# Three more feed-forward channels by seven half-products, in turns with their neighbours; thirteen low parts by adding transfers; the up pairs' weight sums on VectorE

## The chip, the cores and the metric

One core of one Trainium2 chip runs one layer of a hybrid decoder trunk (512 tokens, width 1024, fp32 in and out). The metric is device time of one execution in microseconds (us). A core has a matrix engine (TensorE, PE in the profile, whose weight loads are shown as PEld), a vector engine (VectorE, DVE), a scalar engine (ScalarE, ACT), a general engine (GpSimd, POOL), and SyncE (SP), which here only issues transfers. GpSimd issues transfers too (POOLq in the profile), the adding ones among them: such a transfer adds what it brings to what lies in the target.

## The reference, cut to what matters

```python
def reference(x, ...):
    u = rmsnorm(x, norm1_g)
    a_glu, q, k, v, r, g_low, gate_a, gate_b = split(u @ w_in)
    y_conv = ...          # gated unit, causal convolution of width 31, layer norm, swish, projection
    y_gla = ...           # gated linear attention in chunks of 64, projection
    h = x + (sigmoid(gate_a) * y_conv + sigmoid(gate_b) * y_gla) @ w_o
    u2 = rmsnorm(h, norm2_g)
    z = causal_conv3(u2 @ w_ffn_up) + b          # 2 x 2816 channels, width 3, each channel by itself
    h = h + (silu(z[:, :2816]) * z[:, 2816:]) @ w_ffn_down
    return rmsnorm(h, final_g)
```

The change lies nearly all in the feed-forward part: u2 @ w_ffn_up, the convolution of width 3, the gate, and the product with w_ffn_down.

## The kernel before, in words

**Products in three.** Every fp32 operand is split in a high part (rounded to the matrix engine's type) and a low part (the rest). One product of a 128-row block is three matmuls into the same bank (`mm3`, L448 to L450): activation-high by weight-low, low by high, high by high. A plain weight tile is 128 partitions by 1024 columns, eight blocks of 128, and serves one tile of 128 output channels for 512 tokens: 8 x 3 = 24 matmuls of 512 columns (`col_tile`). In `mm3`'s order the low part of the weight is needed from the first block on.

**How a weight gets ready.** `order` lists all weights in the order of use. SyncE loads each into one of four buffers (`raw_tile`). `weight()` hands over the next one and has the one two places further (`LOOK = 2`) made ready by `split_weight`: ScalarE writes the high part (`whi`, L355 for pairs, L385 for plain tiles), VectorE the low part (`wlo` = raw - high, L356 and L390). Some plain tiles outside the feed-forward part are in the set `ADDED`: for them ScalarE writes not only the high part but also minus the raw tile, rounded, as `wlo` (L387), and an adding transfer issued by GpSimd brings the weight once more onto it (L388), which leaves the low part.

**Seven for eight.** Two weight tiles p and q can be taken as a 2 x 2 matrix of half blocks and multiplied in seven half-size products instead of eight (`two_tiles`, with `step_of_two`): 7 x 4 blocks x 3 = 84 matmuls of 256 columns instead of 48 of 512. In the up stage the two tiles are a channel's value and gate tile (i, 22 + i), in the merge stage two channels of one gate. The operands are called x1 (1024 columns), x3 (1024), x2 (1024) and x4 (512): x1 serves `a11` and `a12`, x3 `n2` and `s1`, x2 `n3` and `s4`, x4 `a22`. Their sums of weights are four additions of 512 columns, made by GpSimd in `two_sums` (L327), three after x1's split and one after x3's, with a third raw buffer for the results. The partial results are copied by ScalarE (`put`, L1178) and combined by VectorE in two working tiles c1 and c2. The activations' side (`up_acts`, seven sums) is made once.

**The feed-forward stages.** 22 channels (tiles of 128) are taken in three groups, `GROUPS`, of four, three and four pairs. For each channel i there are two up tiles, i (value) and 22 + i (gate). Of each, `ffn_conv` makes the convolution of width 3: ScalarE the first tap with the bias (L1497), VectorE the other two (L1500). Then comes silu on ScalarE, and `gated` multiplies on VectorE. The first channel of a pair goes through `first_gated` and `first_of_pair`, the second through `second_of_pair` (VectorE sums L1541, L1542 and splits by `fsplit`, L1520). When a group's channels are there, `seven("w_down", ...)` multiplies them by the down matrix, by seven as well.

In every group, the second channels q of some pairs (6, 7; 10, 11, 21; 14, 15, 18) go by seven, and beside each the first channel f of a following pair (5, 8; 9, 20, 12; 13, 16, 17) by two plain tiles. `up_plan` writes out by hand the order of the two: in the middle of a group, f's two plain tiles a and b are cut in pieces and put between q's operands,

```python
seq = [x1, a1, x3, a2, x2, b1, x4, ("second", q), b2]   # then ("first", f)
```

so q's operands stand with wide products between them. The order of instructions on an engine otherwise follows from a scheduler, with some instructions tied by hand (`issue_after`, `keep_in_program_order`; `third_ahead` ties the making of the next x3 ahead of q's gate).

The merge stage earlier on (gates `w_gb` and `w_ga`, pairs (0, 1) to (6, 7)) uses the same `two_tiles` and `two_sums`.

Of the kernel before, what the change touches and what calls it, by code (L numbers as in the profile page):

```python
# [40 lines left out]
MERGE_REST = [("w_conv", m) for pair in O_PAIRS[2:] for m in pair]  # L41
LOOK = 2

ADDED = {("w_glu", 2 * k) for k in range(2, KT)} | {("w_r", m) for m in range(KT)}
ADDED |= {("w_v", KT // 2 + j) for j in (0, 1)}
RATE = 5.0
# [29 lines left out]
def trunk_layer(ctx: ExitStack, tc: tile.TileContext, a: dict, out: bass.AP):  # L76
# [60 lines left out]
    run64 = cp.tile([P, T], BF16, name="run64")  # L137
# [17 lines left out]

    def up_plan(gi):
# [8 lines left out]
        def unit(q, f, kind):  # L165

            a, b = f, FT + f
            x1, x3, x2, x4 = (("part", q, part) for part in ("x1", "x3", "x2", "x4"))
            a1, a2 = (("tile", a, ks) for ks in halves(4))
            if kind == "opens":  # L170
                b1, b2, b3 = (("tile", b, ks) for ks in halves(4, 6))
                seq = [a1, x1, a2, x3, b1, x2, b2, x4, ("second", q), b3]
            elif kind == "closes":
                a1, a2, a3 = (("tile", a, ks) for ks in halves(3, 6))
                seq = [x1, a1, x3, a2, x2, a3, x4, ("second", q), ("tile", b, whole)]
            else:
                a1, a2 = (("tile", a, ks) for ks in halves(5))
                b1, b2 = (("tile", b, ks) for ks in halves(4))
                seq = [x1, a1, x3, a2, x2, b1, x4, ("second", q), b2]
            return seq + [("first", f)]  # L180
# [143 lines left out]
    def two_sums(name, p, q, part):  # L324

        def add(out, x, y):
            work = nc.gpsimd.tensor_tensor(out, x, y, ALU.add)  # L327
            if name == "w_up":
                tc.keep_in_program_order(work)

        left, right = slice(0, T), slice(T, D)
        if part == "x1":
            one, two = pair_raws[name, p]
            three = raw_tile()
            pair_raws[name, p].append(three)
            add(three[:, left], one[:, left], two[:, left])
            add(three[:, right], three[:, left], two[:, right])
            add(two[:, left], two[:, left], two[:, right])
        if part == "x3":
            one, _, three = pair_raws[name, p]  # L340
            add(three[:, left], three[:, right], one[:, right])

    def split_weight(halves=False, between=None):

        if len(ready) < len(order):
# [4 lines left out]
            if name in SEVEN or name == "two":  # L350
                raw = operand(raw, *spec) if name in SEVEN else two_operand(*spec)
                n = raw.shape[-1]
                hi = wp.tile([P, D], F32R, tag="whi", name=nm("whi"), bufs=4)[:, :n]
                lo = wp.tile([P, D], F32R, tag="wlo", name=nm("wlo"), bufs=4)[:, :n]
                nc.scalar.copy(hi, raw)  # L355
# [18 lines left out]
            if halves:  # L374
# [9 lines left out]
                return [[lambda c=c, part=part: part(c) for c in cols] for part in (high, low)]  # L384
            nc.scalar.copy(hi, raw)  # L385
# [13 lines left out]
    def third_ahead():  # L399

        n = used[0] + LOOK
        if n == len(ready) < len(order) and order[n][0] == "two" and order[n][1][-1] == "x3":
            split_weight()
            return two_low[0]

# [46 lines left out]
    def col_tile(w, acts, acc=None, lo=0, hi=T, at={}, ks=range(KT)):  # L452
# [9 lines left out]
        return acc  # L462

# [707 lines left out]
    def two_tiles(name, p, q, acts7, side_bank, at_once=False):  # L1171

        x, y, z = mm_bank(), side_bank(), side_bank()
        c1, c2 = tmp(), tmp()
# [17 lines left out]
        w = weight("two", (name, p, q, "x3"))  # L1192
        step(x, "n2", w, 1, False)
# [299 lines left out]

    def ffn_conv(acc, m):
# [130 lines left out]
    for gi, pairs in enumerate(GROUPS):  # L1625
# [26 lines left out]
        for what, i, *rest in up_plan(gi):  # L1652
            if what == "tile":
# [3 lines left out]
                col_tile(wt, acts2, acc, ks=rest[0])  # L1657
                if KT - 1 in rest[0] and i < FT:
                    values[i] = value(i, acc)
            if what == "part":  # L1660
                if rest[0] == "x1":
                    units[i] = two_tiles("w_up", i, FT + i, lambda: up_acts, ax_bank)
                done = next(units[i])
                if done:
                    values[i] = value(i, done[0])
                    banks[FT + i] = (None, done[1])
                    third = [taps_at[0], third_ahead()]
# [108 lines left out]
```

## Time and profile before

| | |
|---|---|
| median of 3 runs | 825.51 us (824.53 to 825.88) |
| profiled execution | 826.27 us, of which its span is 824.5 us |
| mean granted TensorE clock | 0.999 |
| TensorE | busy 816.3 us, 99% of the span, 4323 matmuls |
| VectorE | busy 719.2 us, 87%, 1165 instructions |
| ScalarE | busy 449.8 us, 55%, 666 instructions |
| GpSimd | busy 148.9 us, 18%, 133 instructions |
| transfers | 106.27 MB, mean 129 GB/s |

The span is from the first to the last recorded instruction; the execution's own time is 1.8 us longer. A row of the trace gives the start (us), the duration (us), the engine, the line of the program, the operation, output <- inputs by the program's names, and the shapes. A row of a grouped view gives the same without the start, then xcount, the sum of busy time (us) and the mean of one (ns), then the engine's idle time ahead of them and what ended it. Durations of neighbours on one engine overlap a little, so the cost of one in a row is read from the starts.

### The profile page before, as it was taken

Reading aid. Unit: us, or ns where it says so; the run is one execution under the profiler, and the core shown is the slowest. Engines: PE = TensorE matmul, PEld = TensorE weight load, DVE = VectorE, ACT = ScalarE, POOL = GpSimd, SP = SyncE. Lnnn points to the kernel's source line nnn. Section 1 sums busy time; section 2 is a strip of 40 time slices with the busy share of each in tenths; the row PEclk is TensorE's granted clock in tenths of the full one; section 3 lists DMA queues with packets and bytes.
Section 4 is the critical chain, followed back from the end, with each engine's and each line's share of the span. In section 5 each row is a group of like instructions: output and inputs, shape, how many; then the busy total and the mean of one; then the engine's idle time right before and its main releaser. Section 6 shows DMA issues by size and latency. Waiting matters only on the chain.

```text
span 824.5 us, 11562 instructions
## 1 busy us (share of the span) xinstructions
PE 816.3 (99%) x4323; PEld 705.8 (86%) x4323; DVE 719.2 (87%) x1165; ACT 449.8 (55%) x666; POOL 148.9 (18%) x133
## 2 busy tenths in 40 slices
PE   9999999999999999999999999999999999999996
PEld 8888888888888889999988898898889988899885
DVE  5689999998989699886788889989975999789896
ACT  6744446655654456684454546556435663456654
POOL 2000010001010213443001100230123301622012
PEclk9999999999999999999999999999999999999999
DMA  8355673553443103323647633055642457334662
GB/s 317 94 118 150 153 184 103 128 153 103 89 116 103 51 27 114 116 78 106 211 112 215 177 101 103 27 167 160 143 132 89 140 142 164 105 103 148 184 128 103
DMA packets 30616, 106.27 MB, mean 129 GB/s; under 512 B 3464, under 2 KB 3600, under 8 KB 30560
## 3 DMA queue, kind: packets, MB, share of 16 engines
q1 hardware_dynamic: 24784, 85.34, 30.3%
q0 software_dynamic: 5760, 20.19, 14.4%
q8 instruction: 34, 0.56, 0.3%
q14 instruction: 22, 0.18, 0.1%
q10 hardware_dynamic: 16, 0.00, 0.0%
HBM read 103.42 MB, written 2.10 MB: 128 GB/s over the span
## 4 chain that ended last, share of the span: by engine, by line
PE 98%; DMA 0%; ACT 0%; DVE 0%; POOL 0%; POOLq 0%; issue 0%; ACTq 0%
PE mm L448 28%; PE mm L449 28%; PE mm L450 28%; PE mm L662 3%; PE ax L450 2%; PE ax L449 2%; PE ax L448 2%; PE ax L1067 1%; PE ax L576 1%; PE ax L1048 1%; PE ax L1069 1%; PE ax L1035 1%; DMA x<-in_x_dram 0%; PE ax L529 0%; PE ax L1033 0%; PE ax L1082 0%
## 5 line engine op out<-in xcount | busy, mean ns | idle before, releaser
L448 PE MATMUL mm<-uh,wlo 128*128 128x512 f32 (+1 forms) x672 | 244.8, 364 | 0.0
L449 PE MATMUL mm<-ul,whi 128*128 128x512 f32 (+1 forms) x672 | 242.6, 361 | 0.0
L450 PE MATMUL mm<-uh,whi 128*128 128x512 f32 (+1 forms) x672 | 242.3, 361 | 0.0
L450 PEld LDWEIGHTS mm<-uh,whi 128*128 128x128 f32 x672 | 126.9, 189 | 19.4
L448 PEld LDWEIGHTS mm<-uh,wlo 128*128 128x128 f32 x672 | 127.0, 189 | 18.8
L449 PEld LDWEIGHTS mm<-ul,whi 128*128 128x128 f32 x672 | 127.1, 189 | 18.6
L385 ACT CAST whi<-raw 128x1024 fp32r<-128x1024 f32 x86 | 89.7, 1046 | 57.6 <-PE mm L450 29.7
L356 DVE TENSOR_TENSOR wlo<-raw,whi 128x1024 fp32r<-128x1024 f32 x80 | 95.0, 1195 | 24.4 <-ACT whi L355 20.5
L327 POOL TENSOR_TENSOR raw<-raw,raw 128x512 f32<-128x512 f32 x42 | 67.7, 1613 | 211.8 <-DVE wlo L356 116.4
L390 DVE TENSOR_TENSOR wlo<-raw,whi 128x1024 fp32r<-128x1024 f32 x70 | 91.7, 1313 | 14.6 <-ACT whi L385 14.6
L355 ACT CAST whi<-raw 128x1024 fp32r<-128x1024 f32 x80 | 76.3, 957 | 36.2 <-PE mm L450 27.3
L786 DVE SCALAR_TENSOR_TENSOR c<-h,pp,c 128x255 f32<-128x255 f32 (+14 forms) x120 | 57.1, 476 | 3.2 <-ACT c L782 3.0
L786 DVE SCALAR_TENSOR_TENSOR c<-aside,btmp,c 128x255 f32<-128x255 f32 (+14 forms) x120 | 57.1, 476 | 0.0
L786 DVE SCALAR_TENSOR_TENSOR aside<-h,pp,aside 128x255 f32<-128x255 f32 (+6 forms) x112 | 53.3, 476 | 0.0
L355 ACT CAST whi<-kept 128x1024 fp32r<-128x1024 f32 (+1 forms) x32 | 31.8, 996 | 33.6 <-DVE kept L310 16.8
L1500 DVE SCALAR_TENSOR_TENSOR tmp<-mm,pp,tmp 128x511 f32<-128x511 f32 (+1 forms) x56 | 41.4, 743 | 4.0 <-ACT tmp L1497 3.9
L356 DVE TENSOR_TENSOR wlo<-kept,whi 128x1024 fp32r<-128x1024 f32 (+1 forms) x32 | 37.0, 1155 | 5.2 <-ACT whi L355 5.0
L1178 ACT COPY tmp<-mm 128x256 f32<-128x256 f32 x48 | 17.6, 367 | 34.2 <-PE mm L450 33.6
L1416 DVE TENSOR_TENSOR hres<-hres,mm 128x512 f32<-128x512 f32 (+1 forms) x49 | 32.3, 672 | 4.0 <-PE mm L450 2.6
L1497 ACT ACTIVATE tmp<-mm,pp 128x512 f32<-128x512 f32 x28 | 21.8, 777 | 19.1 <-PE mm L450 18.9
L387 ACT ACTIVATE wlo<-raw 128x1024 fp32r<-128x1024 f32 x16 | 16.9, 1059 | 22.1 <-PE mm L448 22.1
L1500 DVE SCALAR_TENSOR_TENSOR tmp<-tmp,pp,tmp 128x511 f32<-128x511 f32 (+1 forms) x32 | 27.8, 887 | 0.4
(351 smaller groups left out, 1782.8 us busy)
## 6 DMA issues: line engine op xcount, KB each, us to landing
raw<-in_w_up_dram SPq DMA_DIRECT2D x44, 512.0 KB, 4.2
raw<-in_w_glu_dram SPq DMA_DIRECT2D x16, 512.0 KB, 4.5
raw<-in_w_down_dram SPq DMA_DIRECT2D x15, 512.0 KB, 4.3
kept<-in_w_down_dram POOLq DMA_DIRECT2D x10, 512.0 KB, 5.8
raw<-in_w_v_dram SPq DMA_DIRECT2D x8, 512.0 KB, 5.8
raw<-in_w_qk_dram SPq DMA_DIRECT2D x8, 512.0 KB, 3.3
raw<-in_w_r_dram SPq DMA_DIRECT2D x8, 512.0 KB, 4.6
wlo<-in_w_r_dram POOLq DMA_DIRECT2D x8, 512.0 KB, 8.2
```

Source lines behind the costliest of these rows:

```text
L327: work = nc.gpsimd.tensor_tensor(out, x, y, ALU.add)
L355: nc.scalar.copy(hi, raw)
L356: two_low[:] = [nc.vector.tensor_tensor(lo, raw, hi.bitcast(F32), ALU.subtract)]
L385: nc.scalar.copy(hi, raw)
L390: pace[0] = nc.vector.tensor_tensor(lo, raw, hi.bitcast(F32), ALU.subtract)
L448: nc.tensor.matmul(acc, ll, rh, start=first, stop=False, **kw)
L449: nc.tensor.matmul(acc, lh, rl, start=False, stop=False, **kw)
L450: nc.tensor.matmul(acc, lh, rh, start=False, stop=last, **kw)
L662: nc.tensor.matmul(acc, act, ready[k // 2][wi][:, j], start=first, stop=last)
L786: nc.vector.scalar_tensor_tensor(out[:, j:], x[:, : half_t - j], w, out[:, j:], ALU.mult, ALU.add)
L1416: done = nc.vector.tensor_tensor(hres[t, n][:, c], hres[t, n][:, c], acc[:, c], op)
L1500: nc.vector.scalar_tensor_tensor(z[:, s:], acc[:, : T - s], w[j], z[:, s:], ALU.mult, ALU.add)
```

## The change

Four things are changed.

1. Channels 5, 9 and 13 (`BOTH`), one in each group, go by seven instead of by two plain tiles. Each was f beside a q that goes by seven already (q = 6, 10 and 14 in that order), and the operands of the two now come in turns: q's x1, f's x1, q's x3, f's x3, q's x2, q's x4, q's gate, f's x2, f's x4, f's gate. Both channels of such a couple get their weight sums in place in the raw buffers, by VectorE (`split_in_place`), so that two raw buffers serve where three did. The set `with_both`, which decides this, holds the numbers of both; `two_tiles` takes its second side bank only at x3 (`lazy`), and the new channel's c1 comes from a room of its own (`seven_room`). `run64` lies in another pool. Such a couple is called a doubled channel in what follows.
2. `two_sums` for the other up pairs runs on VectorE instead of GpSimd; for the merge pairs it stays on GpSimd, but for those that `with_both` names: it is asked by number alone, whatever the matrix.
3. Thirteen plain up tiles join `ADDED`: both tiles of channels 1, 3, 4, 20 and 16, and the value tile of 8, 12 and 17. For them ScalarE negates first, GpSimd issues the adding transfer, and then ScalarE makes the high part.
4. The matmuls of these thirteen go in another order (`high_first`): the sixteen that need only the high part of the weight first, then the eight with its low part.

```diff
...
 BEHIND = [_HALVES[:3], _HALVES[3:6], _HALVES[6:9], _HALVES[9:]]
 BEHIND += [[("w_conv", m, half) for m in pair for half in range(2)] for pair in O_PAIRS[:2]]
 MERGE_REST = [("w_conv", m) for pair in O_PAIRS[2:] for m in pair]
+BOTH = (5, 9, 13)
 LOOK = 2
 ADDED = {("w_glu", 2 * k) for k in range(2, KT)} | {("w_r", m) for m in range(KT)}
 ADDED |= {("w_v", KT // 2 + j) for j in (0, 1)}
+ADDED |= {("w_up", m) for f in (1, 3, 4, 20, 16) for m in (f, FT + f)} | {("w_up", f) for f in (8, 12, 17)}
 RATE = 5.0
 WARM = (6, 3, 2)
 MID = 4
...
     ones = cp.tile([P, P], F32, name="ones")
     mhalf = cp.tile([P, NT], F32, name="mhalf")
     shares = cp.tile([P, P], F32R, name="shares")
-    run64 = cp.tile([P, T], BF16, name="run64")
+    run64 = gp.tile([P, T], BF16, name="run64")
     keep = cp.tile([P, P], U8, name="keep")
     att = gp.tile([P, NT, P], F32, name="att")
...
         nc.gpsimd.memset(att, 0.0)
+    with_both = set(BOTH)
     def up_plan(gi):
...
         def unit(q, f, kind):
+            if f in BOTH:
+                with_both.add(q)
+                turns = ((q, "x1"), (f, "x1"), (q, "x3"), (f, "x3"), (q, "x2"), (q, "x4"), (f, "x2"), (f, "x4"))
+                seq = [("part", i, part) for i, part in turns]
+                return seq[:6] + [("second", q)] + seq[6:] + [("first", f)]
             a, b = f, FT + f
             x1, x3, x2, x4 = (("part", q, part) for part in ("x1", "x3", "x2", "x4"))
             a1, a2 = (("tile", a, ks) for ks in halves(4))
...
     def two_sums(name, p, q, part):
         def add(out, x, y):
-            work = nc.gpsimd.tensor_tensor(out, x, y, ALU.add)
-            if name == "w_up":
-                tc.keep_in_program_order(work)
+            (nc.vector if name == "w_up" else nc.gpsimd).tensor_tensor(out, x, y, ALU.add)
         left, right = slice(0, T), slice(T, D)
         if part == "x1":
...
             one, _, three = pair_raws[name, p]
             add(three[:, left], three[:, right], one[:, right])
+    def split_in_place(hi, lo, name, p, q, part):
+        one, two = pair_raws[name, p]
+        left, right = slice(0, T), slice(T, D)
+        def add(x, y):
+            nc.vector.tensor_tensor(x, x, y, ALU.add)
+        def split(hi, lo, x):
+            nc.scalar.copy(hi, x)
+            two_low[:] = [nc.vector.tensor_tensor(lo, x, hi.bitcast(F32), ALU.subtract)]
+        if part == "x3":
+            split(hi[:, left], lo[:, left], one[:, left])
+            add(one[:, left], two[:, right])
+            add(two[:, left], two[:, right])
+            split(hi[:, right], lo[:, right], one[:, left])
+            add(one[:, right], one[:, left])
+            return
+        split(hi, lo, {"x1": one, "x2": two, "x4": one[:, right]}[part])
+        if part == "x1":
+            add(one[:, left], two[:, left])
     def split_weight(halves=False, between=None):
         if len(ready) < len(order):
...
             raw = raws[len(ready)]
             name, spec = order[len(ready)]
             if name in SEVEN or name == "two":
-                raw = operand(raw, *spec) if name in SEVEN else two_operand(*spec)
-                n = raw.shape[-1]
+                if name == "two" and spec[1] in with_both:
+                    n = T if spec[-1] == "x4" else D
+                else:
+                    raw = operand(raw, *spec) if name in SEVEN else two_operand(*spec)
+                    n = raw.shape[-1]
                 hi = wp.tile([P, D], F32R, tag="whi", name=nm("whi"), bufs=4)[:, :n]
                 lo = wp.tile([P, D], F32R, tag="wlo", name=nm("wlo"), bufs=4)[:, :n]
+                if name == "two" and spec[1] in with_both:
+                    split_in_place(hi, lo, *spec)
+                    ready.append((hi, lo))
+                    refill()
+                    return
                 nc.scalar.copy(hi, raw)
                 two_low[:] = [nc.vector.tensor_tensor(lo, raw, hi.bitcast(F32), ALU.subtract)]
                 with ExitStack() as order_of:
...
                 cols = [slice(j * T, (j + 1) * T) for j in range(2)]
                 return [[lambda c=c, part=part: part(c) for c in cols] for part in (high, low)]
+            if (name, spec) in ADDED and name == "w_up":
+                pace[0] = nc.scalar.mul(lo, raw, -1.0)
+                nc.gpsimd.dma_start(lo, a[name][spec], accum_op=ALU.add)
+                nc.scalar.copy(hi, raw)
+                ready.append((hi, lo))
+                refill()
+                return
             nc.scalar.copy(hi, raw)
             if (name, spec) in ADDED:
                 pace[0] = nc.scalar.mul(lo, raw, -1.0)
...
         if n == len(ready) < len(order) and order[n][0] == "two" and order[n][1][-1] == "x3":
             split_weight()
             return two_low[0]
+    def next_ahead():
+        n = used[0] + LOOK
+        if n == len(ready) < len(order):
+            two = order[n][0] == "two"
+            split_weight()
+            return two_low[0] if two else pace[0]
     two_low = []
...
             if k in at:
                 at[k]()
         return acc
+    def high_first(w, acts, acc, which):
+        every = [(k, 0, p) for k in range(KT) for p in (1, 0)] + [(k, 1, 0) for k in range(KT)]
+        for n in which:
+            k, of_w, of_act = every[n]
+            w_k = w[of_w][:, k * P : (k + 1) * P]
+            nc.tensor.matmul(acc, w_k, acts[k][of_act], start=n == 0, stop=n == len(every) - 1)
     def row_half(name, j0, n, acts, nk, done, tok_inner, middle=None):
...
     combined = []
-    def two_tiles(name, p, q, acts7, side_bank, at_once=False):
-
-        x, y, z = mm_bank(), side_bank(), side_bank()
-        c1, c2 = tmp(), tmp()
+    def two_tiles(name, p, q, acts7, side_bank, at_once=False, lazy=False, room=tmp):
+        x, z = mm_bank(), side_bank()
+        y = None if lazy else side_bank()
+        c1, c2 = room(), tmp()
         t1, t2 = slice(0, H), slice(H, T)
         def put(c, acc):
...
         combine(c1[:, t1], c1[:, t1], z[:, :H], ALU.add)
         yield
         w = weight("two", (name, p, q, "x3"))
+        y = y or side_bank()
         step(x, "n2", w, 1, False)
         put(c2[:, t1], x)
         step(y, "s1", w, 0, True)
...
     heap_scope.close()
     ffn_scope, fp = scoped("ffn", 1)
+    def seven_room():
+        return fp.tile([P, T], F32, tag="c1", name=nm("c1"), bufs=1)
     def ffn_conv(acc, m):
         z = tmp()
         w = [pp[:, PP_FW + m * FW + j : PP_FW + m * FW + j + 1] for j in range(FW)]
...
                 if 0 in rest[0]:
                     banks[i] = (weight("w_up", i), mm_bank())
                 wt, acc = banks[i]
-                col_tile(wt, acts2, acc, ks=rest[0])
+                if ("w_up", i) in ADDED:
+                    high_first(wt, acts2, acc, range(3 * rest[0].start, 3 * rest[0].stop))
+                else:
+                    col_tile(wt, acts2, acc, ks=rest[0])
                 if KT - 1 in rest[0] and i < FT:
                     values[i] = value(i, acc)
             if what == "part":
                 if rest[0] == "x1":
-                    units[i] = two_tiles("w_up", i, FT + i, lambda: up_acts, ax_bank)
+                    units[i] = two_tiles("w_up", i, FT + i, lambda: up_acts, ax_bank, lazy=True, room=seven_room if i in BOTH else tmp)
                 done = next(units[i])
                 if done:
                     values[i] = value(i, done[0])
                     banks[FT + i] = (None, done[1])
-                    third = [taps_at[0], third_ahead()]
+                    if i not in BOTH:
+                        third = [taps_at[0], next_ahead() if i in with_both else third_ahead()]
             if what == "first":
                 w = first_gated(i, values.pop(i), banks.pop(FT + i)[1])
                 if any(i in pair for pair in pairs):
```

## The prediction

> **What bounds the kernel now.** I read the page first (busy shares, the slices, the chain), then the busy time by stretches of the up and down stage, then the order of instructions in time around single products.
>
> ```profile
> span 824.5 us, 11562 instructions
> PE 816.3 (99%) x4323; PEld 705.8 (86%) x4323; DVE 719.2 (87%) x1165; ACT 449.8 (55%) x666; POOL 148.9 (18%) x133
> PE 98%; DMA 0%; ACT 0%; DVE 0%; POOL 0%; POOLq 0%; issue 0%; ACTq 0%
> core 0: us, PE busy (x) PEld busy (x) DVE busy (x) ACT busy (x) POOL busy (x), PEclk, DMA share, GB/s
> 533.00:553.00 20.00, 20.00 (x130) 18.20 (x129) 16.55 (x20) 10.18 (x16) 6.13 (x4) 1.00 0.35 109
> 515.00:604.00 89.00, 89.00 (x473) 77.03 (x472) 81.50 (x104) 47.51 (x64) 17.68 (x14) 1.00 0.49 136
> 604.00:699.00 95.00, 95.00 (x539) 83.48 (x538) 80.91 (x109) 49.54 (x71) 24.13 (x18) 1.00 0.42 117
> 699.00:805.00 106.00, 106.00 (x587) 92.74 (x586) 94.78 (x125) 58.32 (x82) 27.03 (x18) 1.00 0.48 137
> ```
>
> TensorE is the chain: 98% of it, at full clock, with no idle time at all in the three groups of the up and down stage. So time comes only from fewer or shorter TensorE slots, and goes only where TensorE starts to wait. VectorE is second: of the three groups (rows 515, 604, 699) it has 7.5, 14.1 and 11.2 us free. A third party, GpSimd, does little, but see below what it costs VectorE.
>
> **TensorE's gain.** What one slot costs is read from starts of neighbours, since the printed durations overlap.
>
> ```profile
> 562.59 0.40 PE L448 MATMUL mm<-uh,wlo 128*128 128x512 f32 x1
> ...
> 564.65 0.28 PE L448 MATMUL mm<-btmpq,wlo 128*128 128x256 f32 x1
> ...
> 566.07 0.28 PE L448 MATMUL ax<-gainq,wlo 128*128 128x256 f32 x1
> ...
> 567.50 0.40 PE L448 MATMUL mm<-uh,wlo 128*128 128x512 f32 x1
> ...
> 570.32 0.40 PE L448 MATMUL mm<-uh,wlo 128*128 128x512 f32 x1
> ...
> 575.79 0.39 PE L448 MATMUL mm<-whi,yl 128*128 128x512 f32 x1
> ```
>
> From 566.07 to 567.50 stand 12 products of 256 columns: 0.119 us each. From 562.59 to 564.65 stand 9 of 512 columns in a piece of a tile between such products: 0.229 us; from 570.32 to 575.79 a whole plain tile of 24: 0.228 us. An up channel as two plain tiles takes 48 x 0.229 = 10.99 us, by seven 7 x 12 x 0.119 = 10.0 us. Three channels (5, 9, 13) change over: 3 x 0.95 = 2.8 us less. Nothing else shortens TensorE: reordered products of the 13 tiles are the same products.
>
> The Trainium skill, "TensorE: Matmul & The Clock Gate" (section on 56 ns), gives a warm slot as N / 2.4 GHz + 2.5 ns, 215.7 and (worked out) 109.2 ns here; an estimate by it would be 3 x (48 x 215.7 - 84 x 109.2) ns = 3.5 us. The rows are slower than that at both widths, and I take them.
>
> **VectorE: what it gains and loses.** Again by starts of neighbours:
>
> ```profile
> 547.66 1.86 DVE L356 TENSOR_TENSOR wlo<-raw,whi 128x1024 fp32r<-128x1024 f32 x1
> ...
> 557.76 0.74 DVE L1500 SCALAR_TENSOR_TENSOR tmp<-mm,pp,tmp 128x511 f32<-128x511 f32 x1
> 558.41 0.73 DVE L1500 SCALAR_TENSOR_TENSOR tmp<-tmp,pp,tmp 128x510 f32<-128x510 f32 x1
> ...
> 561.00 1.21 DVE L356 TENSOR_TENSOR wlo<-raw,whi 128x1024 fp32r<-128x1024 f32 x1
> 562.13 0.41 DVE L1541 TENSOR_TENSOR v<-v,w 128x256 f32<-128x256 f32 x1
> 562.47 0.68 DVE L1520 TENSOR_TENSOR al<-f,ah 128x512 fp32r<-128x512 f32 x1
> 563.07 0.41 DVE L1542 TENSOR_TENSOR v<-f,v 128x256 f32<-128x256 f32 x1
> ...
> 564.61 0.95 DVE L1520 TENSOR_TENSOR sl<-v,sh 128x768 fp32r<-128x768 f32 x1
> 565.48 0.41 DVE L1530 TENSOR_TENSOR w<-w 128x256 f32<-128x256 f32 x1
> ```
>
> So 1024 columns hold VectorE 1.13 us, 768: 0.87, 512: 0.60, 256: 0.34, a tap of the convolution 0.66. The same low part took 1.86 at 547.66, while GpSimd was adding (rows below). How much that is in all shows in the groups of the up and down stage (from 515 on):
>
> ```profile
> 545.77 2.67 POOL L327 TENSOR_TENSOR raw<-raw,raw 128x512 f32<-128x512 f32 x2 [6.41 <-DMA raw<-in_w_up_dram]
> 548.39 2.28 POOL L327 TENSOR_TENSOR raw<-raw 128x512 f32<-128x512 f32 x1
> ...
> L356 DVE TENSOR_TENSOR wlo<-raw,whi 128x1024 fp32r<-128x1024 f32 x39 | 50.8, 1309 | 12.5 <-ACT whi L355 8.8 <-PE mm L450 3.7
> L390 DVE TENSOR_TENSOR wlo<-raw,whi 128x1024 fp32r<-128x1024 f32 x20 | 28.7, 1433 | 1.8 <-ACT whi L385 1.8
> ...
> L1500 DVE SCALAR_TENSOR_TENSOR tmp<-tmp,pp,tmp 128x510 f32<-128x510 f32 x16 | 16.5, 1032 | 0.4
> ```
>
> Against 1.21 and 0.74 undisturbed: 39 x 0.10 + 20 x 0.22 + 16 x 0.29 = 13 us of VectorE go to GpSimd's 32 adds. They end when the adds move. Now the balance: 11 channels with 4 sums each, 44 x 0.60 = +26.4; three channels get 3 x (3 x 1.13 + 0.67) us of low parts instead of 6 x 1.13, +5.4; their combining, 12 x 0.34 = +4.1; 13 low parts go to transfers, 13 x 1.13 = -14.7; contention -13. Sum +8 us, over three groups with 33 us free. On average VectorE does not become the bound. Here the Trainium skill, "SBUF — State Buffer" (Who interferes with whom), says why moving is nearly free: an add with two SBUF inputs and a GpSimd operation lock each other out of a shared port. The 1.86 against 1.21 agrees.
>
> **The tight place.** The order does. After each doubled channel VectorE must run two convolutions and two gates, then the low part of the next pair's second matrix (x2). I take TensorE's start on the doubled channel as zero. Two channels end at 168 x 0.119 = 20.0. In the second group follow x1 (2.86), 15 wide products (3.43), x3 (2.86), 11 wide (2.52): x2 is due at 31.7; in the first and third by the same sum at 31.2. On VectorE the combine of q's second bank ends at 14.8, soon after TensorE's 14.3. Behind it stand, in the changed program's order of the first two groups: 3 of 1024, 5 of 512, 7 of 256, 8 taps and one of 768 columns: 3.39 + 3.0 + 2.38 + 5.28 + 0.87 = 14.9 us, which gives 29.7. Two waits come on top: 0.9 us for the f channel's own x2 (TensorE at 17.2), 0.7 us for ScalarE, which stands before the next tile's load (its buffer is free at 12.1, it lands 3.2 us later if alone like w_gla's, 4.2 like the other up tiles) and then has the negation and the high part to make, 0.94 us each, before the pass that VectorE waits for:
>
> ```profile
> 323.63 1.04 ACT L385 CAST whi<-raw 128x1024 fp32r<-128x1024 f32 x1
> 324.57 0.36 ACT L1178 COPY tmp<-mm 128x256 f32<-128x256 f32 x1
> ...
> raw<-in_w_up_dram SPq DMA_DIRECT2D x44, 512.0 KB, 4.2
> ...
> kept<-in_w_down_dram POOLq DMA_DIRECT2D x10, 512.0 KB, 5.8
> ...
> wlo<-in_w_r_dram POOLq DMA_DIRECT2D x8, 512.0 KB, 8.2
> ...
> raw<-in_w_gla_dram SPq DMA_DIRECT2D x8, 512.0 KB, 3.2
> ```
>
> I take 3.2, since at 12.1 no other load is on its way, and keep the other end (1.0 us more). x2 is ready at 31.3: 0.1 us late in the first group, 0.4 early in the second. In the third, two more adds stand ahead (16.1 us, one short wait): 31.0, 0.2 early. Three balances of a few tenths, each a sum of 24 steps and some ten hand-overs: I price the waits at 0.2 us each, 0.6 us in all, bounds 0 and 4.5 (1.5 us each, if ScalarE's chain is late by 1.5 more). What follows then is relaxed: the next pairs have 5 us and more.
>
> Between f's x2 and x4 no wide products stand any more: the combine has 1.43 us. By the order VectorE is there at 17.7, due 18.6; in the third group the scheduler put the next x1 between, due 20.4, done 20.2. No term, but no cover either.
>
> **The 13 tiles.** ScalarE gets 13 x 0.94 us more (it is busy 55%), GpSimd 13 issues of 0.9 us; nothing queued behind these waits for them. A low part is read in the last third of its tile. Most have 10 us or more. Two are near: the second half-channel of 20 and of 16, where ScalarE reaches the negation at 31.2 to 31.5 behind the gates, and TensorE reads at 39.2: 7.8 us for a landing that takes 5.8 (kept) or 8.2 (w_r). I take the nearer, kept, which lies in this stage: no wait; the other end costs 2 x 0.4 us.
>
> **More than it says.** The set of doubled channels is filled with 6, 10, 14 beside 5, 9, 13, and is asked by number alone. So the merge pairs (6, 7) of w_gb and w_ga also get their sums in place on VectorE. For w_ga VectorE is not full. For w_gb it is:
>
> ```profile
> 329.69 1.22 DVE L356 TENSOR_TENSOR wlo<-raw,whi 128x1024 fp32r<-128x1024 f32 x1
> ...
> 332.78 0.28 PE L448 MATMUL mm<-sumsq,wlo 128*128 128x256 f32 x1
> ```
>
> Its x2 is ready at 330.9 for 332.8. Four sums (2.4 us) come ahead, about 1.1 us of contention goes: 0.6 us left. No term; up to 0.7 if half of that is wrong.
>
> **Sum.** -2.8 + 0.6 = -2.2 us. The profiled execution took 826.27 us (its span and 1.7 around it), so 824.1; the median of the runs shown is 0.76 lower, 825.51, so 823.3.
>
> **The rivals.** (1) VectorE becomes the bound locally: x2 of the next pair 0.7 to 1.4 us late in each group, because ScalarE's passes, on which 10 of the 24 steps wait, come later than counted. For it: margins of 0.1 to 0.4 us. Against: VectorE idles some 5 us before, waiting for TensorE, and none of the present margins is used up. Waits of 2 to 4 us: 824.7 to 826.9, about no change. (2) Slower: transfers land late. The two low parts at 39.2 are read from GpSimd's queue while the next pair's loads run. If landing takes 10.5 us instead of 5.8, each waits 2.7, and the first third of the next tiles too, about 0.5 us each: 5.4 + 1.0 - 2.2 = +4.2, 829.7; it costs from 7.8 us on and turns the sign at 9. For it: w_r's 8.2. Against: GpSimd's queue is otherwise empty there. (3) TensorE's slots gain more, as the skill's formula has it, without waits: 3.5 us, 822.0. Against: every row.
>
> **Chances.** Forecast 0.48, rival 1 0.28, rival 2 and other local lateness 0.18, rival 3 0.06. A measurement tells 0.2%, 1.65 us, from no change. Faster by that (below 823.86): forecast and rival 3, less a margin, 0.52. Within: 0.27. Slower: 0.21. The range is from a full gain without waits (822.4) to rival 1's upper end (826.9), without the far side of rival 2; the likeliest case alone spans 822.6 to 823.9.
>
> **What would show it.** Right: 256-column products of the doubled channels at 0.119 us, the low part of the next x2 ended within half a microsecond of TensorE's first use, undisturbed 1.21 us low parts, adding transfers landing in under 7.8 us. Wrong: TensorE idle ahead of a doubled channel's x4 or the following x2 with VectorE as releaser, or ahead of the last third of an added tile with a transfer as releaser.

## The result: 0.4% slower

The changed kernel took 828.68 us (median of 5 runs, 827.47 to 830.15), the kernel before 825.51 us (824.53 to 826.35): ratio 1.0039, 95% interval 1.0028 to 1.0050. I forecast 823.3.

The page of the changed kernel, from an execution of 827.47 us; first its span, the busy times and the shares of the chain that ended last, then three rows of its transfers (KB each, median us from issue to landing):

```profile
span 825.8 us, 11855 instructions
PE 814.2 (99%) x4431; PEld 706.3 (86%) x4431; DVE 723.3 (88%) x1227; ACT 473.2 (57%) x705; POOL 95.1 (12%) x106
PE 87%; DVE 5%; DMA 4%; ACT 2%; issue 2%; POOL 0%; POOLq 0%; ACTq 0%; DVEq 0%
raw<-in_w_up_dram SPq DMA_DIRECT2D x44, 512.0 KB, 5.7
raw<-in_w_down_dram SPq DMA_DIRECT2D x15, 512.0 KB, 5.4
wlo<-in_w_up_dram POOLq DMA_DIRECT2D x13, 512.0 KB, 7.3
```

The chain, which was TensorE alone at 98%, now runs through VectorE, transfers and ScalarE for 11%. VectorE is busy only 4 us more. The loads of up tiles land after 5.7 us instead of 4.2. The stretches of the three groups (columns as in the prediction):

```profile
515.00:604.00 89.00, 88.64 (x510) 78.25 (x509) 81.08 (x119) 50.14 (x70) 6.03 (x7) 1.00 0.55 147
604.00:699.00 95.00, 92.46 (x561) 81.50 (x560) 82.12 (x125) 55.06 (x81) 7.75 (x9) 1.00 0.48 124
699.00:805.00 106.00, 105.50 (x623) 93.49 (x622) 96.44 (x145) 64.36 (x94) 7.74 (x9) 1.00 0.59 156
```

VectorE has 7.9, 12.9 and 9.6 us free in them, about as much as before, and TensorE nevertheless stands. Its idle times in order of time, each with what ended it:

```profile
563.88 0.36 PE L503 MATMUL mm<-btmpq,wlo 128*128 128x256 f32 x1 [0.35 <-DVE wlo L396]
644.48 0.36 PE L503 MATMUL mm<-btmpq,wlo 128*128 128x256 f32 x1 [0.74 <-DVE wlo L396]
652.78 0.50 PE L525 MATMUL mm<-uh,wlo 128*128 128x512 f32 x1 [0.56 <-DMA wlo<-in_w_up_dram]
660.46 0.39 PE L503 MATMUL mm<-xq,wlo 128*128 128x256 f32 x1 [0.64 <-ACT tmp L1242]
670.26 0.38 PE L503 MATMUL mm<-uh,wlo 128*128 128x256 f32 x1 [0.37 <-DVE tmp L1245]
684.68 0.50 PE L504 MATMUL mm<-wlo,sh 128*128 128x512 f32 x1 [0.23 <-DVE wlo L396]
746.87 0.50 PE L525 MATMUL mm<-uh,wlo 128*128 128x512 f32 x1 [0.42 <-DMA wlo<-in_w_up_dram]
```

The first two are x2 of channels 7 and 11, the third and the last the low parts of 20b and 16b (the second half-channels of 20 and 16) that came by adding transfers. The printed gaps are shorter than the loss, since the end of a product is modelled and the first slot after a wait is longer (0.34 us behind the one at 652.78, where 0.23 is usual). By starts, less the usual slot, the losses are: x2 0.59 (563.88), 0.98 (644.48) and 0.05 (738.28), together 1.62; transfers 0.83 and 0.70, together 1.53; and behind the first of these 0.90, 0.63, 0.50 and 0.22 (690.6), together 2.25; another 0.34 at 727.30. Sum 5.74. The waits behind the first late landing, 2.25 us, are called the backlog below.

From the first up product to the end of the last product the kernel before took 817.89 - 476.62 = 341.27 us, the changed one 819.11 - 474.89 = 344.22. So 2.95 more, where three channels with 84 half slots in place of 48 whole ones give 2.85 less: 5.8 us of waits, as listed. I compare kernels by this stretch, because the time before it differs between executions: the first up product came at 474.8 to 476.6 us in the profiled ones, and at 474.8 to 476.3 among the changed kernel and its variants, which differ little up to there (last section). Each stage time below is from one execution; that of the changed kernel, 827.47 us, was the fastest of its five. Medians less than some 1.5 us apart are not told apart here.

### The profile page after: what moved, and what is told of

It is laid out like the page before. It is cut to its first block, busy times and chain, and to the rows that moved or that the text cites. A ratio compares the mean times of both kernels' runs of the same rounds, so it can differ in the third digit from the quotient of the medians.

```text
span 825.8 us, 11855 instructions
## 1 busy us (share of the span) xinstructions
PE 814.2 (99%) x4431; PEld 706.3 (86%) x4431; DVE 723.3 (88%) x1227; ACT 473.2 (57%) x705; POOL 95.1 (12%) x106
## 4 chain that ended last, share of the span: by engine, by line
PE 87%; DVE 5%; DMA 4%; ACT 2%; issue 2%; POOL 0%; POOLq 0%; ACTq 0%; DVEq 0%
PE mm L503 23%; PE mm L504 23%; PE mm L505 23%; PE mm L525 5%; PE mm L725 3%; DMA raw<-in_w_up_dram 2%; PE ax L503 2%; PE ax L505 2%; PE ax L504 2%; DVE tmp L1568 2%; DVE wlo L396 1%; DMA wlo<-in_w_up_dram 1%; PE ax L1130 1%; PE ax L1132 1%; PE ax L1111 1%
## 5 line engine op out<-in xcount | busy, mean ns | idle before, releaser
L503 PE MATMUL mm<-uh,wlo 128*128 128x512 f32 (+1 forms) x544 | 192.0, 353 | 0.4 <-DVE tmp L1245 0.4
L505 PE MATMUL mm<-uh,whi 128*128 128x512 f32 (+1 forms) x544 | 189.7, 349 | 0.0
L504 PE MATMUL mm<-ul,whi 128*128 128x512 f32 (+1 forms) x544 | 189.6, 349 | 0.0
L432 ACT CAST whi<-raw 128x1024 fp32r<-128x1024 f32 x67 | 69.9, 1048 | 48.6 <-PE mm L505 31.1
L396 DVE TENSOR_TENSOR wlo<-raw,whi 128x1024 fp32r<-128x1024 f32 (+1 forms) x60 | 68.5, 1151 | 18.2 <-ACT whi L395 18.0
L395 ACT CAST whi<-raw 128x1024 fp32r<-128x1024 f32 (+1 forms) x60 | 57.6, 964 | 30.3 <-PE mm L505 21.3
L437 DVE TENSOR_TENSOR wlo<-raw,whi 128x1024 fp32r<-128x1024 f32 x51 | 63.5, 1249 | 12.2 <-ACT whi L432 12.1
L362 DVE TENSOR_TENSOR wlo<-raw,whi 128x512 fp32r<-128x512 f32 (+1 forms) x40 | 35.5, 903 | 10.4 <-ACT whi L361 10.4
L525 PE MATMUL mm<-uh,whi 128*128 128x512 f32 x104 | 40.6, 391 | 0.0
L525 PE MATMUL mm<-ul,whi 128*128 128x512 f32 x104 | 40.6, 390 | 0.0
L1242 ACT COPY tmp<-mm 128x256 f32<-128x256 f32 x51 | 18.8, 369 | 29.4 <-PE mm L505 29.1
```

Of the source, the lines that this page charges most:

```text
L362: two_low[:] = [nc.vector.tensor_tensor(lo, x, hi.bitcast(F32), ALU.subtract)]
L396: two_low[:] = [nc.vector.tensor_tensor(lo, raw, hi.bitcast(F32), ALU.subtract)]
L437: pace[0] = nc.vector.tensor_tensor(lo, raw, hi.bitcast(F32), ALU.subtract)
L503: nc.tensor.matmul(acc, ll, rh, start=first, stop=False, **kw)
L504: nc.tensor.matmul(acc, lh, rl, start=False, stop=False, **kw)
L505: nc.tensor.matmul(acc, lh, rh, start=False, stop=last, **kw)
```

## Experiments

Theories. **A**: the adding transfers are at fault, which land late beside the loads. **B**: VectorE's order is at fault, which comes too late to x2 behind a doubled channel, and the rest follows from that. Each ratio in the table is to executions of the kernel before taken beside that kernel (medians 825.51 to 825.76 us).

| kernel | median us (range) | ratio to before, 95% | up and down stage, us | to before |
|---|---|---|---|---|
| before | 825.51 (824.53 to 826.35) | | 341.27 | |
| changed | 828.68 (827.47 to 830.15) | 1.0039 (1.0028 to 1.0050) | 344.22 | +2.95 |
| late_low | 824.85 (824.02 to 825.68) | 0.9991 (0.9982 to 1.0000) | 340.80 | -0.47 |
| x2_early | 823.46 (821.92 to 825.04) | 0.9974 (0.9963 to 0.9984) | 338.68 | -2.59 |
| late_low_x2 | 822.03 (821.95 to 824.05) | 0.9960 (0.9948 to 0.9973) | 338.85 | -2.42 |
| no_double | 825.60 (824.84 to 826.72) | 1.0002 (0.9993 to 1.0010) | 342.36 | +1.09 |
| x2_late_neg | 822.25 (822.18 to 823.90) | 0.9966 (0.9953 to 0.9979) | 339.23 | -2.04 |
| late_loads | 827.09 (824.40 to 829.27) | 1.0019 (1.0007 to 1.0032) | 343.52 | +2.25 |
| x2_all_vector | 825.40 (824.69 to 826.59) | 1.0000 (0.9991 to 1.0009) | 341.74 | +0.47 |
| x2_gp_sums | 823.22 (823.11 to 823.85) | 0.9974 (0.9964 to 0.9984) | 339.87 | -1.40 |
| double_only | 833.17 (832.73 to 833.81) | 1.0094 (1.0079 to 1.0110) | 348.69 | +7.42 |
| four_x2 | 828.53 (827.12 to 830.05) | 1.0034 (1.0021 to 1.0047) | 345.34 | +4.07 |
| four | 828.32 (827.68 to 829.22) | 1.0032 (1.0020 to 1.0044) | 344.10 | +2.83 |

**late_low: two adding transfers less.**

```diff
+BY_VECTOR = {("w_up", FT + 20), ("w_up", FT + 16)}
...
-            if (name, spec) in ADDED and name == "w_up":
+            if (name, spec) in ADDED - BY_VECTOR and name == "w_up":
```

> The changed kernel, but the low parts of the second half tiles of channels 20 and 16 are made by VectorE again (2 x 1.13 us), not by adding transfers; the order of their products stays. Theory A (late adding transfers and what they set off): in the trace of the changed kernel the two late landings cost 0.8 and 0.7 us, and the backlog behind the first (loads of the next tiles at 8.5 us, ScalarE idle for 5 us, then three more waits) another 2.2; all of that goes: 828.7 - 3.7 = 825.0. Theory B (VectorE's order behind the doubled channels is the cause of everything, the landings only add to it): two more low parts on VectorE at the fullest place; the direct 1.5 us go, the other waits stay or grow: 827 to 829. The x2 waits of 0.6 and 1.0 us stay in both.

3.42 us of the stage go, as theory A had it (3.7): the two late landings and nearly all that followed the first. The median, 824.85, is A's 825.0; B's 827 to 829 didn't come. The x2 waits stay (0.35 and 0.88 us printed).

**x2_early: x2's low part ahead on VectorE, and the negation ahead with it on ScalarE.**

```diff
             if what == "first":
-                w = first_gated(i, values.pop(i), banks.pop(FT + i)[1])
+                with ExitStack() as order_of:
+                    if i in BOTH:
+                        prefetch(4)
+                        order_of.enter_context(tc.issue_after(two_low[0].ins))
+                    w = first_gated(i, values.pop(i), banks.pop(FT + i)[1])
```

> The changed kernel with the next pair's x3 and x2 split asked for ahead of the doubled channel's second gate, and that gate's VectorE work tied behind x2's low part, which so moves forward by some 2.5 us on VectorE; in the same order ScalarE's negation for 20b and 16b moves forward by 2 to 3 us too. Theory B: the x2 waits (0.6, 1.0 and 0.1 us) go and so does what follows: 824 to 825. Theory A: the three waits go (-1.65), and the earlier negation lets the transfers land in time, -1.5 and the backlog's -2.2: 823.3; if the landings come late in spite of it, 827.0.

5.54 of the 5.8 us go. The median, 823.46, lies nearer to A's 823.3 than to B's 824 to 825, but these are too close to decide by. In the second group VectorE's rows of the changed kernel and then of x2_early:

```profile
638.76 0.69 DVE L1588 TENSOR_TENSOR al<-f,ah 128x512 fp32r<-128x512 f32 x1 [0.74 <-ACT ah L1587]
...
641.84 0.69 DVE L1582 TENSOR_TENSOR w<-tmp,tmp 128x512 f32<-128x512 f32 x1
642.44 0.42 DVE L1245 TENSOR_TENSOR tmp<-tmp,ax 128x256 f32<-128x256 f32 x1
642.77 0.42 DVE L1598 TENSOR_TENSOR w<-w 128x256 f32<-128x256 f32 x1
643.11 1.82 DVE L396 TENSOR_TENSOR wlo<-raw,whi 128x1024 fp32r<-128x1024 f32 x2
```

```profile
638.32 0.69 DVE L1588 TENSOR_TENSOR al<-f,ah 128x512 fp32r<-128x512 f32 x1 [0.89 <-ACT ah L1587]
638.93 0.42 DVE L1610 TENSOR_TENSOR v<-f,v 128x256 f32<-128x256 f32 x1
639.27 1.22 DVE L396 TENSOR_TENSOR wlo<-raw,whi 128x1024 fp32r<-128x1024 f32 x1
```

x2's low part (643.11, the first of the two) stood behind a tap, a weight sum, a split, the gate `w`, a combine and a subtraction; it now starts at 639.27, and none of those makes TensorE wait when it comes later. VectorE does the same work, and even waits longer for ScalarE. This edit moves two things, since the adding transfer of 20b goes out earlier too: 165.25 us after the first up product, 168.62 in the changed kernel.

**late_low_x2: both.** The two edits together.

> Both edits: low parts of 20b and 16b by VectorE, and x2's low part ahead of the doubled channel's second gate. Theory A and theory B together: nothing but the bank wait of 0.3 us in the third group stays, 828.7 - 1.65 - 1.5 - 2.2 = 823.3. If the two low parts fill VectorE at this place: a new wait at x4 or at the plain tile, 824 to 826.

No gain over x2_early in the stage (338.85 against 338.68); the medians, 1.4 us apart, are not told apart. With x2 early, the adding transfers of 20b and 16b cost nothing that shows. It is the lowest median of all, 0.9960 of before and 0.8% under the changed kernel; x2_late_neg below is level with it.

**no_double: the rest of the change without the doubling** (`BOTH = ()`).

> The changed kernel without the doubled channels (5, 9 and 13 by two plain tiles again): TensorE has its 2.85 us back, the 13 adding transfers, the other products' order and the weight sums on VectorE stay. Theory A: what is wrong is the adding transfers beside the loads: some of the late landings stay, 827 to 830. Theory B: only the couple's order is wrong; without it nothing waits: 825.5, as before. Theory C (the sums on VectorE fill it): waits all over the up stages, 828 or more.

1.09 us more than before in the stage, no change in the median, which is what B said. None of TensorE's waits in the stage ends with a transfer, although an adding transfer among them took 8.8 us (at 642.81). The adding transfers and the sums on VectorE gain nothing by themselves.

So both A's and B's edit remove the backlog. The next two ask how it hangs together.

**x2_late_neg: x2 early, the negation late.** The negation and its adding transfer of 20b and 16b are held until x4's high part has been issued, where the changed kernel had them. The lines come on top of x2_early's.

```diff
+            if (name, spec) in HELD:
+                nc.scalar.copy(hi, raw)
+                def negated():
+                    nc.scalar.mul(lo, raw, -1.0)
+                    nc.gpsimd.dma_start(lo, a[name][spec], accum_op=ALU.add)
+                held.append(negated)
...
-                nc.scalar.copy(hi, raw)
+                high = nc.scalar.copy(hi, raw)
+                while held:
+                    with tc.issue_after(high.ins):
+                        held.pop()()
```

> As x2_early (x2's low part forward on VectorE, 823.5), but ScalarE's negation for 20b and 16b, with its adding transfer, is held back to where the changed kernel had it, behind the high part of x4. Nothing else moves on ScalarE. Theory A (the landing is a cause by itself): the read of 20b's low part is 0.9 us earlier than in the changed kernel and the landing is not, so TensorE waits 1.5 us there, some 0.6 at 16b, and the backlog (2.2) comes back: 826.5 to 828. Theory B (the backlog came from VectorE being late): two waits of about 1 us each at most, no backlog: 824.5 to 825.5.

Theory A falls as far as it took the late transfer for a cause by itself: the transfer goes out as late as before (at 644.39; at 643.51 in the changed kernel, whose stage began 1.45 us sooner), but lands in 7.6 us instead of 9.2, and TensorE loses 0.14 us. B was right that no backlog comes, but 822.25 is under its 824.5 to 825.5 as well. The transfers around it, first of the changed kernel (that of 20b and the load behind it, at 643.5 to 644.5, then that of 20a and the load behind it, at 629.8), then of x2_late_neg (that of 20b at 644.4, and the load just before):

```profile
wlo<-in_w_up_dram POOLq DMA_DIRECT2D x1, 512.0 KB, 9.2
raw<-in_w_up_dram SPq DMA_DIRECT2D x1, 512.0 KB, 8.6
...
wlo<-in_w_up_dram POOLq DMA_DIRECT2D x1, 512.0 KB, 6.0
raw<-in_w_up_dram SPq DMA_DIRECT2D x1, 512.0 KB, 7.2
```

```profile
wlo<-in_w_up_dram POOLq DMA_DIRECT2D x1, 512.0 KB, 7.6
raw<-in_w_up_dram SPq DMA_DIRECT2D x1, 512.0 KB, 3.9
```

**Theory D**: the loads. There are four raw buffers, and x2's comes free when VectorE has made its low part. In the changed kernel SyncE issues the next two loads 0.38 us ahead of the adding transfer and 0.85 us behind it (643.13 and 644.36; x2's low part ends at 644.33), so that three transfers of 512 KB are on their way at once. In x2_late_neg they go out 3.42 and 0.38 us ahead. Theory D says that the late buffer brings the collision, and the collision the backlog.

**late_loads: x2's low part early, its raw buffer late.**

```diff
+                if name == "two" and spec[0] == "w_up" and spec[1] in (11, 15) and spec[-1] == "x2":
+                    reader.append(nc.vector.tensor_copy(small(1, "var"), raw[:, :1]))
...
-        nc.vector.tensor_tensor(w[:, T:], w[:, :H], w[:, H:T], ALU.subtract)
+        last = nc.vector.tensor_tensor(w[:, T:], w[:, :H], w[:, H:T], ALU.subtract)
+        while reader:
+            tc.add_manual_dep(reader.pop().ins, last.ins.name, ...)   # issued behind last
```

> x2_late_neg with one more reader of x2's raw buffer for channels 11 and 15: VectorE copies a single column of it behind the last subtraction of the doubled channel's second gate, where the changed kernel had x2's low part. So x2's low part stays early, but the raw buffer comes free as late as in the changed kernel, and the loads that wait for it go out some 2.5 us later. Theory D (the late buffer makes the loads fall on the adding transfer, and the backlog comes from there): the landing at 20b takes 9 us again, a wait of 0.8 to 1.6 us there, the next tile's load 8.5 us, waits of some 2 us behind: 825 to 826.5. Theory E (the backlog came from VectorE's own lateness): no such waits, 822.3 to 823.

Theory D's chain comes back. One copy of one column (0.15 us, at 644.25) brings 4.3 us back into the stage. The loads go out at 642.47 and 643.30, that is 0.37 us ahead of the adding transfer and 0.46 behind it, and were handed other buffers (the one that the negation frees at 642.44, and x4's at 643.27). Counted from the first up product, the adding transfer goes out at 168.05 us in both kernels and the loads at 167.68 and 168.51, where x2_late_neg has 164.63 and 167.67. So the load behind lands 4.9 us later: 0.8 from going out later, 4.0 from taking 8.0 us instead of 3.9. At 20b TensorE loses 1.19 us by starts. The median, 827.09, is even above what I expected (825 to 826.5), and its executions spread over 4.9 us, where the starts of the profiled ones differ by 1.9: the collision does not seem to cost the same each time. Its rows: the wait of TensorE, ScalarE's wait for the load of the next tile, and the landings of the adding transfer and of that load:

```profile
651.49 0.50 PE L543 MATMUL mm<-uh,wlo 128*128 128x512 f32 x1 [0.91 <-DMA wlo<-in_w_up_dram]
...
651.38 1.06 ACT L442 ACTIVATE wlo<-raw 128x1024 fp32r<-128x1024 f32 x1 [2.87 <-DMA raw<-in_w_up_dram]
...
wlo<-in_w_up_dram POOLq DMA_DIRECT2D x1, 512.0 KB, 8.6
raw<-in_w_up_dram SPq DMA_DIRECT2D x1, 512.0 KB, 8.0
```

The same row of ScalarE in the changed kernel shows how the backlog begins: it stands 5.05 us for the next tile's raw load, and the high parts and the copies out of TensorE's banks (L1242, the releaser at 660.46) stand behind it.

```profile
653.02 1.06 ACT L426 ACTIVATE wlo<-raw 128x1024 fp32r<-128x1024 f32 x1 [5.05 <-DMA raw<-in_w_up_dram]
```

One reserve: the added copy also moved a few neighbours on VectorE (the sums of the next pair by some 5 us, set against the adding transfer), which I didn't separate.

A second limit: the collision is not enough by itself. x2_early has it too, with loads 0.38 us ahead of the adding transfer of 20b and 0.33 behind; the load ahead and the adding transfer:

```profile
raw<-in_w_up_dram SPq DMA_DIRECT2D x1, 512.0 KB, 3.7
wlo<-in_w_up_dram POOLq DMA_DIRECT2D x1, 512.0 KB, 8.2
```

The load behind took 6.3 us. But all three go out over 3 us sooner than in the changed kernel; 20b's low part lands at 648.43, 2.1 us ahead of its first use, and ScalarE waits 0.60 us for the next tile where it waited 5.05. How much is left is open: in four_x2 (below), with the same order in this group, the two took 9.5 and 9.0 us, and TensorE lost some 1.3 us behind. What costs is the collision when it comes late; x2_early gains time against it and doesn't prevent it.

**Is the relief of VectorE needed?** Three kernels: x2_all_vector (x2_early, all 13 low parts by VectorE again), x2_gp_sums (late_low_x2, the sums of the five channels by seven that aren't doubled back on GpSimd), and double_only (the changed kernel with both taken back and no x2 edit).

> x2_early with all 13 low parts made by VectorE (13 x 1.13 = 14.7 us more there, no adding transfer for an up tile); their products' order stays. If VectorE's room is what the balance says (33 us free, 8 + 14.7 used), the three groups still fit and only the places near the couples cost: 823.5 to 825. If VectorE is the bound in a group: 826 or more. If the adding transfers were only a burden: as late_low_x2, 822.0, or less.

> late_low_x2 (822.0) with the weight sums of the five channels by seven that are not doubled back on GpSimd (20 additions of 512 columns; 20 x 0.60 = 12 us less on VectorE, against 20/32 of 13 = 8 us lost to contention). By that balance no change that can be measured: 821.5 to 823. If GpSimd's additions (2.3 to 2.7 us each) make x3 late or disturb VectorE at the couples: 823.5 to 826.

> The changed kernel with only the doubling left: all 13 low parts by VectorE, the other channels' sums on GpSimd; the order on VectorE behind the couples as the scheduler has it (no x2 edit). TensorE -2.85. Theory A (transfers cost 3.4 of 5.8): 825.5 - 2.85 + 1.65 for the x2 waits = 824.3. If VectorE is too full without the relief (some 11 us more than in the changed kernel): the x2 waits grow and tiles wait too, 827 to 831.

With x2 early, the adding transfers are worth 3.06 us of the stage (341.74 against 338.68), nearly all in the first group; the row is x2 of the first couple. The median, 825.40, lies between what I had for a fit and for a bound. The sums on VectorE are worth 1.02 (339.87 against 338.85), one wait of 1.1 us at 721.84; the medians, 1.2 us apart, don't tell the two apart. Without either, and without the x2 edit, x2 of channel 7 alone waits 2.1 us; for this kernel I expected 824.3 if transfers were the trouble and 827 to 831 if VectorE was too full, and it was worse than both. Their rows, x2_all_vector first:

```profile
545.02 0.36 PE L496 MATMUL mm<-btmpq,wlo 128*128 128x256 f32 x1 [1.68 <-DVE wlo L362]
```

```profile
569.24 0.36 PE L498 MATMUL mm<-btmpq,wlo 128*128 128x256 f32 x1 [2.14 <-DVE wlo L398]
```

**A fourth doubled channel** (`BOTH = (5, 9, 13, 16)`), on x2_early (four_x2) and on late_low_x2 (four):

> x2_early with one more doubled channel, 16 beside 15 in the last group (its two tiles leave the adding transfers). TensorE another 0.95 us less; VectorE 3 x 1.13 + 0.67 + 1.4 + 1.2 = 6.6 us more in a group that has the least room behind 13 and 14: 821.5 to 822.5 if its waits stay under 1 us; 823.5 to 827 if x2 and x4 of the second couple come late.

> late_low_x2 with the same further doubled channel 16 beside 15: 821.1 (822.0 - 0.95) if VectorE keeps up, 823 to 827 if it doesn't.

Both miss, and lie above even the upper ends: the last group has no room for a couple right behind a couple. Of four's 6.3 us of waits, by starts, 6.2 are there. In four, the doubled channel waits for its own low parts:

```profile
732.29 0.39 PE L504 MATMUL mm<-xq,wlo 128*128 128x256 f32 x1 [1.58 <-DVE wlo L363]
```

## Why the prediction was wrong

In short: the sum was -2.8 us of products and +0.6 of waits. The products came out, but the waits were 5.8 us.

- **TensorE's gain, -2.8**: right. x2_early shows 2.59 of 2.85 in the stage; the rest I did not trace. The prediction's own figures, 10.99 less 10.0, give 0.99 for a channel and not 0.95, and a full gain without waits gives 822.7 and not 822.4; neither changes anything here.
- **VectorE's balance, +8 us of 33 free, no bound on average**: right that the average is no bound, but the size was too high. Over the whole stage VectorE is busy 4.0 us more (303.15 and 307.11), half of what I had; six of the 13 tiles, those of channels 1, 3 and 4, lie ahead of the three stretches in which I counted the room. VectorE keeps 30 us free in these, and its low parts are undisturbed again: the one at 547.87 took 1.22 us, its counterpart at 547.66 in the kernel before 1.86, beside GpSimd's additions. That a VectorE operation with both inputs in SBUF contends with a GpSimd operation that reads SBUF is what the Trainium skill, "SBUF — State Buffer" (Who interferes with whom), says; 1.86 against 1.22 agrees.

```profile
547.87 1.22 DVE L396 TENSOR_TENSOR wlo<-raw,whi 128x1024 fp32r<-128x1024 f32 x1
```

- **The tight place, x2 of the next pair, 3 x 0.2 us**: the place was right, the size not: 0.59, 0.98 and 0.05. I had x2 ready 31.3, 31.3 and 31.0 us after the start of the couple; it was 31.7, 32.5 and 31.5 (563.73 - 532.03, 644.33 - 611.79, 738.11 - 706.62). From there to TensorE's start it is another 0.15 us (563.73 to 563.88), which I had left out. That the third place cost next to nothing was luck: x2 was 0.5 us later than I had it, but due only at 31.6 instead of 31.2. The largest error, 1.2 us in the second group, contains a hand-over that I had not counted: ScalarE's high part of 20b stood before the split of f, its load had gone out beside the adding transfer of 20a and took 7.2 us, and VectorE waited 0.74 us (638.76 above; the other half microsecond is not traced):

```profile
637.16 1.05 ACT L428 CAST whi<-raw 128x1024 fp32r<-128x1024 f32 x1 [1.50 <-DMA raw<-in_w_up_dram]
638.12 0.61 ACT L1587 CAST ah<-f 128x512 fp32r<-128x512 f32 x1
```

- **The 13 tiles, no wait (other end 2 x 0.4)**: wrong, 0.83 and 0.70. I took the 5.8 us that transfers took in the kernel before for 20b and 16b; they took 9.2 and 7.6, and that of 16b went out 1.1 us later than I had it (739.19 - 706.62 = 32.6).
- **"What follows then is relaxed"**: this is the step that failed most, 2.25 us in the second group. I put what follows a late x2 or a late landing at nothing. I asked of a late VectorE only what TensorE waits for, not which buffer it frees late and which load that puts beside which transfer. Theory D is that chain: x2's raw buffer free at 644.33, the next load out at 644.36 beside the adding transfer, landed 8.6 us later, and ScalarE standing 5.05 us for it. Without the two adding transfers (late_low) or with x2 early (x2_late_neg) it is gone, and with the loads late again (late_loads) it is back.
- **Rival 2** (829.7, two landings of 10.5 us and 0.5 us behind each) was nearest in outcome and had half of the mechanism; the adding transfer is needed for it (late_low), but isn't enough by itself (x2_late_neg). **Rival 1** gave 2 to 4 us of waits at x2, where 1.62 stood.
- **The merge pairs**: no cost, as said; TensorE doesn't wait there.

## What to carry to other kernels

A margin of a few tenths of a microsecond on an engine's order is no margin: count also which buffers the late instruction frees, which loads wait for these, and what else is on its way when they go out. Where such an engine idles on average, first look whether the urgent instruction can be issued ahead of work that nobody waits for; here that one edit turned +0.4% into -0.3%, with the same work. Adding transfers are not free transfers: the loads of up tiles took 5.7 us with the thirteen, and 4.2 in x2_all_vector and double_only, which have none of them, as before the change.

## What the hardware showed that I had not expected

Three transfers of 512 KB at once: the adding one took 9.2 us and the load behind it 8.6, where the loads of w_gla took 3.2 and those of up tiles in the kernel before 4.2. With a load just ahead and none behind (x2_late_neg) the adding one took 7.6 and that load 3.9. So such a collision costs the adding transfer and the load behind it most, though SyncE issued the one and GpSimd the other. The Trainium skill, "DMA: Bandwidth & Descriptors" (Issuing engines are not separate DMA queues), says that all of them run on the same 16 engines and interleave; the longer landings agree.

The start of an execution is not the same each time. The same 16 small products near the start (128 columns) took 424 ns each in the profiled execution of before, 292 in that of late_low_x2, and in x2_late_neg TensorE stood 1.2 us at 25 us, which that of before didn't:

```profile
L576 PE MATMUL ax<-ident,x 128*128 128x128 f32 x16 | 3.9, 424 | 0.5 <-DMA x<-in_x_dram 0.5
```

```profile
L640 PE MATMUL ax<-ident,x 128*128 128x128 f32 x16 | 2.3, 292 | 0.3 <-DMA x<-in_x_dram 0.3
```

```profile
25.28 1.09 PE L654 MATMUL ax<-ident,x 128*128 128x128 f32 x8 [1.20 <-ACT x L712]
```

Starts of such products go from 0.21 us apart to 0.11 at 5.0 us in late_low_x2, at 6.4 in the changed kernel and past 10.1 in before. The moment at which they double their pace was another in each of these three executions; the granted clock in the profile reads 1.00 in the slow part too (before, 4 to 8 us).
